# Fused matmul and RMS norm: a new order of evictions, copies and scalings at the end of the head, and a later scaling of row block 3

## The chip, the cores and the metric

The kernel runs on one core of one Trainium2 chip. The metric is device time in microseconds (us) of one execution. The engines are named as in the profile: PE is TensorE's matmuls and PEld its weight loads, DVE is VectorE, ACT is ScalarE, POOL is GpSimd, SP is SyncE, which here only issues DMAs.

## The reference

With a and b of 2048 x 2048 in float32, gamma of 2048 elements:

```python
x = np.matmul(a, b)
rms = np.sqrt(np.mean(x ** 2, axis=-1, keepdims=True) + eps)
return (gamma * x / rms).astype(np.float32)
```

Every row of the product is divided by its own root mean square, so a row can be scaled only when all of its 2048 columns are computed.

## The kernel before

The rows of a are cut into 16 blocks of 128 (0 to 15), the columns of b into halves of 1024 and chunks of 512. Blocks 0 to 3 are the **head**; they are multiplied while b is still being loaded. Blocks 4 to 15 follow in six **groups** of two row blocks (group 2 holds blocks 4 and 5, group 3 blocks 6 and 7, and so on), each worked off in two halves of b's columns. A group's half is computed with seven products instead of eight (a Strassen scheme in Winograd's form): a product is 8 matmuls of 128x128 by 128x512 into one PSUM bank, and its operands are sums and differences of quarters of a and b. The sums of b are made once, in the head (`b_diff`, `b_rest`); those of a once per group by `a_sums` on DVE (L323 to L330): sum 1 in place, sum 2 from sum 1, sum 3 from sum 2, sum 4 later. Product 7 uses sum 3, product 6 sum 2, product 5 sum 1, product 3 sum 4.

A row block from 4 on goes through these steps before PE can use it:

- `load_block` (L129) or `load_half`: a DMA on POOL's queue into one of two buffers of 1 MB. Block b uses the buffer of block b - 2, so its load cannot start before that block's scaling. `load_after` (L548) puts a one-element copy (L140) ahead of a load on POOL, which waits until a given transposed block has landed.
- `row_norm` (L217): two squares with a sum on ACT (L221) and a root (L224).
- `row_factor` (L227) and `row_apply` (L238) on DVE: four tiny operations that make a power of two, then one operation of 128x2048 (L240) that scales the block to float16.
- Transposing: blocks 4 and 5 on PE (`transpose_half`, L185, eight transposes of 128x128 into one bank), each half copied from PSUM by `take_transposed` (L195) on ACT or DVE; all later blocks by a DMA transposition on SP's queue (`transpose_dma`, L198).

The results go to tiles x of 128x1024. Products of the head's second pair of blocks (2 and 3) end in `pair_ends` (L505); plain products of blocks 0 and 1 are evicted by `evict` (L400). When a block's row is complete, `square_right` (L291) squares the right half on ACT and takes the root, to which `take_pre` (L276) has added the earlier part on DVE; `finish` (L301) then scales both halves with the inverse and gamma on DVE (L306, one per half) and stores each on SP's queue (L309).

Nothing here is scheduled by a planner: the program's order is the order of every engine's queue, and each engine works its queue strictly in order. What an instruction waits for, all behind it on its engine waits for too.

The places that the change touches:

- the head's end, L474 to L503: the last evictions of blocks 0 and 1, the norms and scalings of blocks 4 and 5, the products 6, 3, 5 and 4 of blocks 2 and 3 (right half), the transposes of blocks 4 and 5 and the first sums of group 2;
- `first_segment` (L552), the first half of group 2, where the load of block 8 is issued;
- `segment` (L578), where segment 1 (the second half of group 2) scales blocks 2 and 3 and makes the sums of group 3, which segment 2 needs first in its product 6.

PSUM has eight banks: tbank and acc_0 to acc_6; in the head's end acc_0 to acc_3 hold the plain products, u2 is acc_4, u4 acc_5, p7 acc_6.

Of the kernel before, what the change touches and what calls it, by code (L numbers as in the profile page):

```python
# [17 lines left out]
def kernel(  # L18
# [13 lines left out]
    nc = tc.nc  # L32
# [3 lines left out]
    KT = K // P  # L36
# [6 lines left out]
    HB = 4  # L43
    NG = MB // 2
    G0 = HB // 2
# [12 lines left out]
    tbank = psum.tile([P, CH], FP32, name="tbank")  # L58
    acc = [psum.tile([P, CH], FP32, name=f"acc_{n}") for n in range(7)]
# [22 lines left out]
    def a16_slot(mb):  # L82
        if mb == HB + 1:
            return a16_first
        if mb == HB:
            return x_slot[2 * HB - 1].bitcast(FP16)
        return head_flat.bitcast(FP16)[:, (2 + mb % 2) * K:(3 + mb % 2) * K]
# [3 lines left out]
    def at(mb):  # L91
        return (at_even, at_odd)[(mb // 2) % 2][:, mb % 2]
# [4 lines left out]
    def add(out, in0, in1, op=ALU.add):  # L97
        nc.vector.tensor_tensor(out=out, in0=in0, in1=in1, op=op)  # L98
# [30 lines left out]
    def load_block(mb):  # L129
        a32[mb] = a_pool.tile([P, K], FP32, name="a32")  # L130
        nc.gpsimd.dma_start(out=a32[mb], in_=a[mb * P:(mb + 1) * P, :])
# [53 lines left out]
    def transpose_half(mb, h, bank):  # L185
        view = bank.bitcast(FP16).rearrange("p (g m) -> p g m", m=P)
        for n in range(8):
            kt = h * 8 + n
            nc.tensor.matmul(
                view[:, n, :], a16[mb][:, kt * P:(kt + 1) * P], identity_h,  # L190
                is_transpose=True, start=(n == 0), stop=(n == 7),
            )
        return view

    def take_transposed(mb, h, view, copy):  # L195
        copy(out=at(mb)[:, h * 8:(h + 1) * 8, :], in_=view)
# [9 lines left out]
    def new_msq(mb):  # L206
        msq[mb] = msq_pool.tile([P, NCH + 1], FP32, name="msq")
        n_sq[mb] = 1
# [18 lines left out]
    def row_factor(mb):  # L227
        s = stat_pool.tile([P, 1], FP32, name="s")
        nc.vector.tensor_scalar_max(out=s, in0=norm.pop(mb), scalar1=1e-18)
        nc.vector.reciprocal(out=s, in_=s)  # L230
        nc.vector.tensor_single_scalar(out=s.bitcast(I32), in_=s.bitcast(I32),
                                       scalar=0x7F800000, op=ALU.bitwise_and)
        new_msq(mb)
        nc.vector.tensor_scalar(out=msq[mb][:, 0:1], in0=s, scalar1=s, scalar2=float(eps),
                                op0=ALU.mult, op1=ALU.mult)
        factor[mb] = s

    def row_apply(mb):  # L238
        a16[mb] = a16_slot(mb)
        nc.vector.tensor_scalar_mul(out=a16[mb], in0=a32.pop(mb), scalar1=factor.pop(mb))  # L240
# [29 lines left out]
    def square_half(mb, h):  # L270
        square_of(mb, x_tile(mb, h))
# [4 lines left out]
    def take_pre(mb):  # L276

        pre_of[mb] = stat_pool.tile([P, 1], FP32, name="pre")
        add(pre_of[mb], msq[mb][:, 0:1], msq[mb][:, 1:2])

    def root(last, part):
        rms = stat_pool.tile([P, 1], FP32, name="rms")
        nc.scalar.activation(out=rms, in_=last, func=ACTF.Sqrt, bias=part, scale=1.0)  # L283
        return rms
# [6 lines left out]
    def square_right(mb):  # L291

        square_half(mb, 1)
        rms_of[mb] = root(msq[mb][:, 2:3], pre_of.pop(mb))
# [6 lines left out]
    def finish(mb, order=(0, 1)):  # L301
        if mb not in inverse_of:
            inverse_of[mb] = inverse(rms_of.pop(mb))
        for h in order:
            x = x_half.pop((mb, h))
            nc.vector.scalar_tensor_tensor(  # L306
                out=x, in0=x, scalar=inverse_of[mb], in1=gamma_sb[:, h * HALF:(h + 1) * HALF],
                op0=ALU.mult, op1=ALU.mult)
            nc.sync.dma_start(out=rows(mb, h * HALF, (h + 1) * HALF), in_=x)  # L309
# [35 lines left out]
    def product_matmul(g, j, m, bank, kp, start):  # L345
        lhsT = {1: lambda: quarter(g, 0, 0), 2: lambda: quarter(g, 0, 1),
                3: lambda: sum_of(g, 4), 4: lambda: quarter(g, 1, 1), 5: lambda: sum_of(g, 1),
                6: lambda: sum_of(g, 2), 7: lambda: sum_of(g, 3)}[m]()
        rhs = {1: lambda: b_quarter(j, kp, 0, 0), 2: lambda: b_quarter(j, kp, 1, 0),
               3: lambda: b_quarter(j, kp, 1, 1), 4: lambda: sums[j][:, 2, kp, :],  # L350
               5: lambda: b_quarter(j, kp, 0, 1), 6: lambda: sums[j][:, 0, kp, :],
               7: lambda: sums[j][:, 1, kp, :]}[m]()
        nc.tensor.matmul(bank, lhsT[:, kp, :], rhs, start=(start and kp == 0),  # L353
                         stop=(kp == KP - 1), skip_group_check=not start)
# [45 lines left out]
    def evict(groups, engines):  # L400
        for g, engine in zip(groups, engines):
            copy_on(engine)(out=x_chunk(*g), in_=banks[g])  # L402
# [22 lines left out]
    plain = [(r, c) for r in range(2) for c in (2, 3)]  # L425
# [43 lines left out]
    r2, r3 = HB - 2, HB - 1  # L469
# [4 lines left out]
    b_rest(1, KP - 1)  # L474
    evict(plain[:2], "AD")
    row_norm(HB)
    for r in range(HB):
        take_pre(r)
    row_norm(HB + 1)
    product(PAIR, 1, 6, u2, start=False)  # L480
    nc.vector.tensor_copy(out=u4, in_=u2)
    evict(plain[2:3], "D")
    row_factor(HB)
    row_apply(HB)
    product(PAIR, 1, 3, acc[0])
    product(PAIR, 1, 5, u4, start=False)
    row_factor(HB + 1)
    row_apply(HB + 1)
    evict(plain[3:], "A")
    square_right(0)  # L490
    turned = [transpose_half(HB, 0, tbank)]
    for kp in range(KP):
        product_matmul(PAIR, 1, 4, u2, kp, False)
        if kp == 4:
            turned.append(transpose_half(HB, 1, acc[1]))
    load_block(HB + 3)
    take_transposed(HB, 0, turned[0], nc.scalar.copy)
    turned += [transpose_half(HB + 1, h, bank) for h, bank in enumerate((tbank, acc[2]))]
    square_right(1)
    take_transposed(HB, 1, turned[1], nc.vector.tensor_copy)  # L500
    take_transposed(HB + 1, 0, turned[2], nc.vector.tensor_copy)
    take_transposed(HB + 1, 1, turned[3], nc.scalar.copy)
    a_sums(G0, (3, 1, 2), False)  # L503

    def pair_ends():  # L505
# [42 lines left out]
    def load_after(src, mb):  # L548
        wait_for(src)
        load_block(mb)  # L550

    def first_segment():  # L552
        n, g, j = 0, G0, 0
        nxt = 2 * g + 2
        do(n, 1)
        do(n, 7, False)
        finish(0, (1,))
        pair_ends()
        do(n, 2)
        row_norm(nxt)  # L560
        a_sums(g, (4,))
        finish(0, (0,))
        do(n, 6)
        do(n + 1, 1)
        prepare(nxt)
        do(n, 5)
        nc.scalar.copy(out=chunks(n)[2], in_=B7)
        take(n, 22)
        row_norm(nxt + 1)
        take(n, 11)  # L570
        finish(1)
        do(n, 4)
        prepare(nxt + 1)
        load_after(at(nxt)[:, KT - 1, 0:1], nxt + 2)
        take(n, 21)
        square_half(2 * g + 1, j)

    def segment(n):  # L578
        g, j = halves[n]
        ra, rb, nxt = 2 * g, 2 * g + 1, 2 * g + 2  # L580
        more = g + 1 < NG
        do(n, 6)
        if j == 0:
            finish(ra - 1)
            if more:
                row_norm(nxt)
        elif g == G0:
            square_right(r2)
        do(n - 1, 3)
        take(n - 1, 12)  # L590
        if j == 0:
            square_right(ra - 2)
            if more:
                prepare(nxt)
            a_sums(g, (4,))
            finish(ra - 2)
        else:
            square_half(ra, 0)
            if g == G0:
                square_right(r3)  # L600
                for r in (r2, r3):
                    finish(r, (1, 0))
        do(n, 2)
        take(n, 11)
        do(n + 1, 1)
        if j == 0 and more:
            row_norm(nxt + 1)
        if j == 1 and g + 2 < NG:
            load_after(at(nxt + 1)[:, KT - 1, 0:1], nxt + 3)
        if j == 1 and more:  # L610
            a_sums(g + 1, (1, 2))
        do(n, 7)
        if j == 1 and more:
            a_sums(g + 1, (3,))
        do(n, 5)
        take(n, 22)
        if j == 1:
            take_pre(rb)
            take_pre(ra)
        do(n, 4)  # L620
        take(n, 21)
        if j == 0:
            square_half(rb, 0)
            if more:
                prepare(nxt + 1)
            if g + 2 < NG:
                load_after(at(nxt)[:, KT - 1, 0:1], nxt + 2)
        else:
            square_right(rb)

    def last_group():
        n = len(halves) - 2
# [137 lines left out]
```

## Time and profile before

| what | value |
|---|---|
| median of 3 runs | 226.18 us (225.19 to 226.31) |
| the profiled execution's own time | 224.53 us |
| its span, first to last instruction | 222.8 us |
| PE busy | 208.4 us, 94% |
| DVE busy | 144.6 us, 65% |
| ACT busy | 116.2 us, 52% |
| granted TensorE clock, mean | 0.992 |

Times in the timeline count from the span's start. A row of the timeline gives start, length, engine, line of the code, operation, what it writes and reads, how many instructions are merged, and in brackets the engine's idle time just before with what ended it. Matmuls are pipelined: a product's row is 1.89 us long, but the next product starts 1.72 to 1.73 us behind it; the distance of starts is what counts. A releaser is the one that came last by the profile.

### The profile page before, as it was taken

Reading aid. Unit: us, or ns where it says so; the run is one execution under the profiler, and the core shown is the slowest. Engines: PE = TensorE matmul, PEld = TensorE weight load, DVE = VectorE, ACT = ScalarE, POOL = GpSimd, SP = SyncE. Lnnn points to the kernel's source line nnn. Section 1 sums busy time; section 2 is a strip of 40 time slices with the busy share of each in tenths; the row PEclk is TensorE's granted clock in tenths of the full one; section 3 lists DMA queues with packets and bytes.
Section 4 is the critical chain, followed back from the end, with each engine's and each line's share of the span. In section 5 each row is a group of like instructions: output and inputs, shape, how many; then the busy total and the mean of one; then the engine's idle time right before and its main releaser. Section 6 shows DMA issues by size and latency. Waiting matters only on the chain.

```text
span 222.8 us, 2900 instructions
## 1 busy us (share of the span) xinstructions
PE 208.4 (94%) x1012; PEld 97.2 (44%) x1032; DVE 144.6 (65%) x281; ACT 116.2 (52%) x229; POOL 38.5 (17%) x74
## 2 busy tenths in 40 slices
PE   7799999999999999599999999999999999999970
PEld 3345544444444444244444444444444444444440
DVE  2128678999987994879616980678337963483381
ACT  2110003900797548569744965297726964364782
POOL 8544434433020011200110010200010000000030
PEclk9999999999999999999999999999999999999996
DMA  7999999999928489996885599547874875062044
GB/s 154 172 202 207 203 206 210 210 210 253 420 68 359 170 243 278 351 290 233 288 235 191 197 273 282 188 185 197 284 103 186 206 258 94 1 266 116 0 183 193
DMA packets 36719, 46.59 MB, mean 209 GB/s; under 512 B 22240, under 2 KB 26336, under 8 KB 35424
## 3 DMA queue, kind: packets, MB, share of 16 engines
q0 software_dynamic: 10608, 23.86, 43.9%
q1 hardware_dynamic: 25824, 22.29, 32.6%
q10 hardware_dynamic: 272, 0.26, 0.3%
q8 instruction: 8, 0.13, 0.2%
q14 instruction: 7, 0.06, 0.1%
HBM read 34.60 MB, written 16.78 MB: 231 GB/s over the span
## 4 chain that ended last, share of the span: by engine, by line
PE 53%; ACT 1%; issue 1%; DVE 1%; ACTq 0%
PE acc L353 53%; ACT sq L718 0%; ACT sq L267 0%; ACT a L645 0%; DVE s L330 0%; ACTq L765 0%; DVE head_at L330 0%; ACT rms L283 0%; DVE r L288 0%
## 5 line engine op out<-in xcount | busy, mean ns | idle before, releaser
L267 ACT ACTIVATE sq<-x 128x1024 bf16<-128x1024 f32 (+1 forms) x33 | 33.2, 1005 | 31.3 <-DVE x L98 27.5
L353 PEld LDWEIGHTS <-s 128*128 128x128 f16 (+1 forms) x312 | 30.4, 98 | 39.9 <-DVE s L330 3.5
L366 PE MATMUL acc<-b,head_at 128*128 128x512 bf16 x171 | 42.3, 379 | 1.5 <-DMA b<-in_b_dram 1.3
L353 PE MATMUL acc<-b,head_at 128*128 128x512 bf16 x164 | 40.8, 379 | 0.3
L306 DVE SCALAR_TENSOR_TENSOR x<-x,r,gamma_sb 128x1024 f32<-128x1024 f32 x28 | 34.8, 1282 | 0.5
L353 PE MATMUL acc<-b,at_even 128*128 128x512 bf16 x142 | 33.3, 379 | 0.1
L353 PEld LDWEIGHTS <-head_at 128*128 128x128 f16 (+1 forms) x216 | 21.0, 98 | 25.0
L353 PEld LDWEIGHTS <-at_even 128*128 128x128 f16 x192 | 18.8, 98 | 22.4
L353 PE MATMUL acc<-early,s 128*128 128x512 bf16 x108 | 27.1, 379 | 0.2
L366 PEld LDWEIGHTS <-head_at 128*128 128x128 bf16 x176 | 16.9, 97 | 20.6 <-issue 1.5
L221 ACT ACTIVATE sq<-a 128x1024 bf16<-128x1024 f32 x24 | 25.3, 1054 | 0.5
L353 PE MATMUL acc<-t_left,s 128*128 128x512 bf16 x95 | 22.5, 379 | 2.6 <-DVE s L330 2.4
L353 PE MATMUL acc<-b,s 128*128 128x512 bf16 x103 | 24.4, 379 | 0.1
L112 POOL DMA_DIRECT2D b<-in_b_dram x32 | 17.2, 541 | 20.6 <-DMA b<-in_b_dram 14.6
L98 DVE TENSOR_TENSOR x<-acc,x 128x512 f32<-128x512 f32 x23 | 15.9, 689 | 6.1 <-ACT x L534 3.3
L402 ACT COPY x<-acc 128x512 f32<-128x512 f32 x6 | 3.5, 583 | 25.6 <-PE acc L366 25.6
L240 DVE TENSOR_SCALAR head_at<-a,s 128x2048 f16<-128x2048 f32 x10 | 12.8, 1277 | 0.0
L288 DVE RECIPROCAL r<-rms 128x1 f32<-128x1 f32 x16 | 2.6, 161 | 12.8 <-ACT rms L283 12.7
L530 ACT COPY acc<-acc 128x512 f32<-128x512 f32 x12 | 6.9, 578 | 7.3 <-PE acc L353 7.3
L181 DVE COPY head_at<-tbank 128x1024 bf16<-128x1024 bf16 x7 | 4.8, 692 | 9.0 <-PE tbank L176 9.0
L330 DVE TENSOR_TENSOR at_even<-at_even 128x1024 f16<-128x1024 f16 x3 | 2.1, 692 | 12.5 <-DMA at_even<-head_at 12.5
L140 POOL CAST pace<-head_at 128x1 f32<-128x1 f16 x4 | 2.5, 620 | 43.6 <-DMA head_at<-head_at 43.6
(104 smaller groups left out, 208.1 us busy)
## 6 DMA issues: line engine op xcount, KB each, us to landing
out_dram<-x SPq DMA_DIRECT2D x29, 512.0 KB, 3.3
a<-in_a_dram POOLq DMA_DIRECT2D x10, 1024.0 KB, 5.9
b<-in_b_dram POOLq DMA_DIRECT2D x32, 256.0 KB, 10.1
a<-in_a_dram POOLq DMA_DIRECT2D x4, 512.0 KB, 9.8
early<-in_a_dram POOLq DMA_DIRECT2D x7, 256.0 KB, 10.2
gamma_sb<-in_gamma_dram POOLq DMA_DIRECT2D x2, 512.0 KB, 9.9
out_dram<-x SPq DMA_DIRECT2D x3, 256.0 KB, 2.5
out_dram<-a SPq DMA_DIRECT2D x1, 768.0 KB, 3.3
```

The source lines that it names most:

```text
L98: nc.vector.tensor_tensor(out=out, in0=in0, in1=in1, op=op)
L112: nc.gpsimd.dma_start(out=raw[j][kp][:, t, :], in_=b[lo:lo + P, j * HALF:(j + 1) * HALF])
L181: nc.vector.tensor_copy(out=head_at[:, 2 * kp:2 * kp + 2, :, :], in_=view)
L221: nc.scalar.activation(out=junk, in_=a32[mb][:, h * HALF:(h + 1) * HALF], func=ACTF.Square, scale=2.0 ** -8, accum_out=n2[:, h:h + 1])
L240: nc.vector.tensor_scalar_mul(out=a16[mb], in0=a32.pop(mb), scalar1=factor.pop(mb))
L267: nc.scalar.activation(out=sq[:, 0:src.shape[-1]], in_=src, func=ACTF.Square, scale=inv_sqrt_n, accum_out=msq[mb][:, c:c + 1])
L288: nc.vector.reciprocal(out=r, in_=rms)
L306: nc.vector.scalar_tensor_tensor(out=x, in0=x, scalar=inverse_of[mb], in1=gamma_sb[:, h * HALF:(h + 1) * HALF], op0=ALU.mult, op1=ALU.mult)
L353: nc.tensor.matmul(bank, lhsT[:, kp, :], rhs, start=(start and kp == 0), stop=(kp == KP - 1), skip_group_check=not start)
L366: nc.tensor.matmul(bank, head_at[:, kt, r, :], head_rhs(c, kt), start=(kt == 0), stop=(kt == KT - 1))
L402: copy_on(engine)(out=x_chunk(*g), in_=banks[g])
L530: nc.scalar.copy(out=b2, in_=b1)
```

## The change

At the head's end four things move:

- the four `take_pre` operations go from ahead of u4's copy on DVE to behind the copy of block 4's second half;
- the eviction of the third plain bank (`plain[2]`) goes from DVE, ahead of block 4's factor, to ACT, behind both norms; that of the fourth goes on ACT between the two `square_right`;
- the factor and scaling of block 5 follow those of block 4 directly in the program;
- block 4 is transposed in one go ahead of product 4, and block 5 within it (halves after 4 and 6 of its 8 matmuls), with both of its copies on DVE; before, block 4's second half lay within product 4 and block 5 behind it, with one copy on ACT.

In group 2, row block 3's `finish` moves from the middle of segment 1, ahead of the sums of group 3, to the end of that segment. In the first segment the load of block 8 waits for block 7's transposition in place of block 6's. No instruction is added or removed on any engine; only the order changes, and the engine of two copies (one from DVE to ACT, one from ACT to DVE).

```diff
     evict(plain[:2], "AD")
     row_norm(HB)
-    for r in range(HB):
-        take_pre(r)
     row_norm(HB + 1)
     product(PAIR, 1, 6, u2, start=False)
     nc.vector.tensor_copy(out=u4, in_=u2)
-    evict(plain[2:3], "D")
-    row_factor(HB)
-    row_apply(HB)
+    for mb in (HB, HB + 1):
+        row_factor(mb)
+        row_apply(mb)
+    evict(plain[2:3], "A")
     product(PAIR, 1, 3, acc[0])
     product(PAIR, 1, 5, u4, start=False)
-    row_factor(HB + 1)
-    row_apply(HB + 1)
+    turned = [transpose_half(HB, h, (tbank, acc[1])[h]) for h in range(2)]
+    take_transposed(HB, 0, turned[0], nc.scalar.copy)
+    take_transposed(HB, 1, turned[1], nc.vector.tensor_copy)
+    load_block(HB + 3)
+    for r in range(HB):
+        take_pre(r)
+    square_right(0)
     evict(plain[3:], "A")
-    square_right(0)
-    turned = [transpose_half(HB, 0, tbank)]
+    square_right(1)
     for kp in range(KP):
+        if kp in (4, 6):
+            h = kp // 2 - 2
+            view = transpose_half(HB + 1, h, (tbank, acc[2])[h])
+            take_transposed(HB + 1, h, view, nc.vector.tensor_copy)
         product_matmul(PAIR, 1, 4, u2, kp, False)
-        if kp == 4:
-            turned.append(transpose_half(HB, 1, acc[1]))
-    load_block(HB + 3)
-    take_transposed(HB, 0, turned[0], nc.scalar.copy)
-    turned += [transpose_half(HB + 1, h, bank) for h, bank in enumerate((tbank, acc[2]))]
-    square_right(1)
-    take_transposed(HB, 1, turned[1], nc.vector.tensor_copy)
-    take_transposed(HB + 1, 0, turned[2], nc.vector.tensor_copy)
-    take_transposed(HB + 1, 1, turned[3], nc.scalar.copy)
     a_sums(G0, (3, 1, 2), False)
...
@@ first_segment
         prepare(nxt + 1)
-        load_after(at(nxt)[:, KT - 1, 0:1], nxt + 2)
+        load_after(at(nxt + 1)[:, KT - 1, 0:1], nxt + 2)
         take(n, 21)
...
@@ segment
             if g == G0:
                 square_right(r3)
-                for r in (r2, r3):
-                    finish(r, (1, 0))
+                finish(r2, (1, 0))
         do(n, 2)
...
         else:
             square_right(rb)
+            if g == G0:
+                finish(r3, (1, 0))
```

## The prediction

> **What bounds the kernel now.** I read the busy table first, then the chain of work that ended last, then the list of waits, then the timeline around each place where TensorE (PE) stood still.
>
> ```profile
> PE 208.4 (94%) x1012; PEld 97.2 (44%) x1032; DVE 144.6 (65%) x281; ACT 116.2 (52%) x229; POOL 38.5 (17%) x74
> ```
>
> PE is busy 94% of the span; no other engine is near. The chain, in order of time (start, length, what):
>
> ```profile
> 93.16 0.60 DVE head_at L330
> ...
> 93.85 0.70 DVE s L330
> ...
> 94.60 9.46 PE acc L353 x43
> 104.05 0.05 issue
> 104.11 10.74 PE acc L353 x49
> ```
>
> From 94.60 to the final product PE runs without a wait (each further piece repeats "10.74 x49" with 0.05 between). So whatever moves PE's start at 94.60 moves the end, as long as nothing behind it becomes late. Ahead of 94.60 the chain is on VectorE (DVE), making operand sums. The waits (total, times, longest) name the gap:
>
> ```profile
> PE acc L353 <- DVE s L330: 2.4, 1, 2.4
> ```
>
> Around it, in the timeline:
>
> ```profile
> 83.60 0.53 POOL L131 DMA_DIRECT2D a<-in_a_dram  x1
> 83.69 5.01 SPq L199 DMA_TRANSPOSE head_at<-head_at  x1
> ...
> 90.27 1.89 PE L353 MATMUL acc<-early,at_even 128*128 128x512 bf16 x7
> ...
> 90.68 2.48 DVE L306 SCALAR_TENSOR_TENSOR x<-x,r,gamma_sb 128x1024 f32<-128x1024 f32 x2
> ...
> 93.07 0.68 DVE L330 TENSOR_TENSOR head_at<-head_at 128x1024 f16<-128x1024 f16 x1
> ```
>
> A product is 8 matmuls; neighbours start 1.725 us apart (88.54, 90.27). The next product should start at 90.27 + 1.725 = 92.00; it starts at 94.60: **2.60 us lost**. It needs sum 2 of blocks 6 and 7, two L330 operations. These start at 93.07, straight behind the scaling of row block 3 (L306, twice 1.28 us). Block 7's transposition (issued 83.69) landed at 91.2, so it was there by then. The head's end is the other place:
>
> ```profile
> 61.39 0.68 DVE L402 COPY x<-acc 128x512 f32<-128x512 f32 x1
> ...
> 61.67 1.89 PE L353 MATMUL acc<-b,head_at 128*128 128x512 bf16 x7
> ...
> 62.69 1.28 DVE L240 TENSOR_SCALAR x<-a,s 128x2048 f16<-128x2048 f32 x1
> ...
> 62.95 0.30 ACT L224 ACTIVATE norm<-n 128x1 f32<-128x1 f32 x1
> ...
> 64.02 0.62 PE L189 MATMUL tbank<-identity_h,x 128*128 128x128 f16 x8 [0.46 <-DVE s L229]
> ...
> 67.55 1.89 PE L353 MATMUL acc<-b,at_even 128*128 128x512 bf16 x7
> 67.75 1.01 ACT L196 COPY at_even<-acc 128x1024 f16<-128x1024 f16 x1 [0.38 <-PE acc L189]
> ...
> 69.54 1.90 PE L353 MATMUL acc<-t_left,s 128*128 128x512 bf16 x8
> ```
>
> Product 5 starts at 61.67 and frees PE at 63.39; the transposes of block 4 start at 64.02, when its scaling (L240, ends 63.97) is done: 0.63 us lost. The group's first product frees PE at 67.55 + 1.725 = 69.27; product 7 starts at 69.54, behind the copy of block 5 on ScalarE (ACT): 0.27 lost.
>
> **The change, part by part.**
>
> *DVE ahead of block 4.* Four L98 sums of 128x1 (60.52 to 60.79) and one eviction (0.60 to the next start) leave this place. The copy of u2 starts when the eviction at 59.92 is through, about 60.52 instead of 60.79. Factor 4 then starts 0.60 later, at 61.12 (norm 4 is there at 60.70), its scaling 0.70 after that, at 61.82, ending at 63.10. That is ahead of 63.39, so the 0.63 us stall goes. What is late next is block 5: its factor now meets norm 5, ready at 62.95 + 0.30 = 63.25, so it starts at 63.28 (before 63.88), scales from 63.98, and ends at 65.26.
>
> *PE.* Sixteen transposes of block 4 at 0.455 per eight: 63.39 to 64.30. Four matmuls of product 4 (0.216 each): to 65.17. Block 5's first half waits for 65.26 + 0.05 = 65.31: a new wait of 0.14, and queued behind it is all of PE. ScalarE's copy out of tbank (64.06 to 65.05) is done by then. Then 0.455, 0.43, 0.455, 0.43: product 4 ends at 67.08. Transposes between matmuls of an open accumulation are in the old trace too (65.56, pitch undisturbed), so I cost them at nothing beyond their time. The group's first product starts at 67.08 against 67.55: **0.47 gained**.
>
> *The copies.* DVE does block 4's second half at 65.17 to 65.86, the four moved sums to 66.1, block 5's first half at 66.05 (PE done 65.92) and its second at 66.84 (PE done 66.80) to 67.53. Sum 3 runs 67.55 to 68.24, product 7 wants it at 67.08 + 1.725 = 68.81. The 0.27 goes: **PE is 0.73 us ahead** from here (68.81 against 69.54). If the cover of 0.5 us is gone, that part comes back one for one. ACT has the moved eviction at 63.16, where it did another of 0.56 us before; its queue (copy 0.99, square and root 1.4, eviction 0.5, square and root 1.4) ends at about 68.4, and its next work waits for PE at 69.0. Nothing there is late. POOL's loads of blocks 6 and 7 follow the two scalings and move some 0.6 us forward.
>
> One row speaks against this stretch: the load of block 6 took 1.47 us to issue at 64.51, beside the scaling at 64.58, where its like take 0.53. The Trainium skill, "SBUF — State Buffer", section "SBUF: two separate sides", says that a VectorE operation in a two-port mode and GpSimd writing DMA descriptors shut each other out, whoever comes first. By it a load issued first could hold block 5's scaling 0.5 us, and the gain would be 0.5 us less; the row has that scaling at its usual 0.13 us behind its factor, so I charge nothing to DVE.
>
> *Row block 3's scaling behind the first group's last products.* This takes 0.20 + 2.48 us of DVE from ahead of the sums. Row block 2's scaling ended at 89.99; its cause is a chain over PE, DVE and ACT that moves with PE, so about 89.3. Sums 1 and 2 take 0.75 each: sum 2 at 90.8. PE wants it at 92.00 - 0.73 = 91.27. **All 2.60 us go**, if block 7 has landed by about 89.7.
>
> *The load of block 8* moves from ahead of block 7's transposition to behind its landing. The old trace has it at 83.60, with the transposition at 83.69, which took 7.5 us to land; the others took 4.3 to 6.8 (4.3 to 5.0 where no load ran beside them, 5.3 to 6.8 where one did). Without the load I take 4.3 to 5.5 (two stores are still in flight); the scaling of block 7 ends some 0.7 us earlier, so issue is near 82.95 and landing at 87.3 to 88.5. Loads 8 and 9 then go out together at about 88.5, where load 9 was at 91.95. Loads of 1 MB landed in 5.1 to 7.9 us: block 8 at 93.6 to 96.4. ACT reaches its squares at about 95.0 (98.67 before, of which 3.7 us go with the wait ahead of it). Late by nothing to 1.4 us; queued behind on ACT are the copies and squares of that segment. Their slack: the next products that wait for that chain are product 6 of the next half (copy ended 104.26, used 106.70) and product 6 of group 4 (sum 2 at 117.63, used 118.78). Shifted by 3.33 us, block 8 may be as late as 96.5 before PE waits. I take zero.
>
> *The scaling of block 3 at its new place* occupies DVE 93.0 to 95.6 and pushes the scaling of block 5 to 98.2; the norm of block 8 comes at 97.7. At most 0.6 us, under the slack above. Zero.
>
> **Sum.** 0.47 + 0.26 + 2.60 = 3.33 us. The profiled execution took 224.53 us with a span of 222.8, so 221.2 with 219.5. It is faster than all three timed runs; taken off their median: 226.18 - 3.33 = **222.9 us**.
>
> **Rivals.** (a) *Both stalls go*: 222.9, in 222.2 to 223.5. (b) *The transposition of block 7, or the chain to block 2's scaling, is the next wait.* For: without the move, landing at 82.95 + 7.5 = 90.45 gives sum 2 at 91.95, 0.7 late; block 2's scaling unmoved would give 0.2 to 0.7 late. Price 0.2 to 1.5: 223.1 to 224.6. (c) *Loads 8 and 9 collide with the stores of blocks 2 and 3* (windows 87 to 95 already move 331 to 360 GB/s): block 8 at 97 to 99, 0.5 to 2.5 lost: 223.4 to 225.4. (d) *The change doesn't do what it says*: sums still late by something not in the old trace (the 0.73 alone stays): 225.4. In the compiled order the sums stand ahead of block 3's scaling, so this is small. (e) *Slower*: load 8's wait on ACT is one for one behind 96.5, so it turns the sign at 96.5 + 3.33 = 99.8, that is 11.3 us after issue. The longest median landing of a group is 10.2 us, in the loading phase with many loads queued. At 102 it would be 226.18 - 3.33 + 5.5 = 228.4. By the skill's "TensorE: Matmul & The Clock Gate", "What's actually happening", an idle window of 3.4 us halves PE's clock; the 2.4 us gap here left it at 1.00, and no run here shows the longer one, which would come on top of (e).
>
> **How the numbers follow.** (a) 0.63, (b) 0.15, (c) 0.12, (d) 0.04, (e) 0.06. About 0.5% (1.1 us) is what timing can tell from no change, so faster means under 225.05: (a), (b) and two thirds of (c), 0.86; same 0.09; slower 0.05. The range 221.9 to 225.0 holds (a), (b) and most of (c), with some spread between runs.
>
> **What would show it.** In the new profile PE should not wait for L330; product 6 of group 3 should start near 91.3, behind its predecessor by 1.7; block 7 should land in under 6 us; ACT's squares of block 8 near 95 with no DMA named as releaser. A wait of ACT for the load of block 8 of over 1.5 us, followed by a PE wait for a copy or sum, would prove me wrong, as would a PE wait of over 0.3 us for block 5's scaling.

## The result, and the profile after

| | before | after |
|---|---|---|
| median | 225.69 us (4 runs, 224.59 to 226.31) | 223.12 us (4 runs, 222.88 to 223.24) |
| ratio, with its 95% interval | | 0.989 (0.9845 to 0.9935) |
| profiled execution, span | 222.8 us | 221.1 us |
| mean granted clock, profiled | 0.992 | 0.996 |

The forecast was 222.9 us, in a range of 221.9 to 225.0. Most executions of the kernel before, here and beside the experiments, fall into two groups, near 224.4 us at a mean granted clock of 0.991 to 0.995 and near 226.2 us at 0.984 to 0.987; the four of the changed kernel form one group, at 0.990 to 0.996. The two profiled means in the table differ only by the last fortieth of the span (0.6 and 0.8 there by the pages), where no matmul is left.

The profile after the head's end, in the timeline (start, length, engine, line, operation):

```profile
61.97 1.28 DVE L240 TENSOR_SCALAR x<-a,s 128x2048 f16<-128x2048 f32 x1
...
63.60 0.61 PE L189 MATMUL tbank<-identity_h,x 128*128 128x128 f16 x8
...
63.80 0.53 POOL L131 DMA_DIRECT2D a<-in_a_dram  x1 [8.98 <-DVE s L229]
...
64.18 1.28 DVE L240 TENSOR_SCALAR a_first<-a,s 128x2048 f16<-128x2048 f32 x1
...
65.52 0.62 PE L189 MATMUL tbank<-identity_h,a_first 128*128 128x128 f16 x8
...
67.29 1.89 PE L353 MATMUL acc<-b,at_even 128*128 128x512 bf16 x7
...
69.01 1.89 PE L353 MATMUL acc<-t_left,s 128*128 128x512 bf16 x8
```

This execution reached product 5 of the head at 61.87, 0.20 us later than the one before (61.67), so 0.20 is to be taken off. Block 4's transposes start 1.73 us behind product 5, without the wait of 0.63. Block 5's first half waits 0.17 for its scaling. Product 7 starts at 69.01 - 0.20 = 68.81, against 69.54: the 0.73 us of the forecast, at the very time it named.

At the start of group 3:

```profile
83.15 1.69 SPq L199 DMA_TRANSPOSE head_at<-head_at  x1
...
86.97 2.48 DVE L306 SCALAR_TENSOR_TENSOR x<-x,r,gamma_sb 128x1024 f32<-128x1024 f32 x2
...
88.25 0.53 POOL L131 DMA_DIRECT2D a<-in_a_dram  x1
...
89.37 0.69 DVE L330 TENSOR_TENSOR head_at<-head_at 128x1024 f16<-128x1024 f16 x1
...
89.73 1.89 PE L353 MATMUL acc<-early,at_even 128*128 128x512 bf16 x7
90.15 0.69 DVE L330 TENSOR_TENSOR s<-head_at 128x1024 f16<-128x1024 f16 x1
...
91.46 1.89 PE L353 MATMUL acc<-t_left,s 128*128 128x512 bf16 x8
```

Sum 1 follows the scaling of row block 2 directly, and product 6 starts 1.73 us behind its predecessor: the whole 2.60 us are gone here. But the list of waits still has one of PE for a sum:

```profile
ACT sq L221 <- DMA a<-in_a_dram: 1.2, 1, 1.2
PE acc L353 <- DVE s L330: 1.0, 1, 1.0
```

It is at another place, one group later:

```profile
96.21 1.06 ACT L221 ACTIVATE sq<-a 128x1024 bf16<-128x1024 f32 x1 [1.18 <-DMA a<-in_a_dram]
...
100.95 3.78 SPq L199 DMA_TRANSPOSE at_even<-head_at  x1
...
103.55 1.89 PE L353 MATMUL acc<-early,s 128*128 128x512 bf16 x8
...
104.89 1.49 DVE L98 TENSOR_TENSOR x<-acc,x 128x512 f32<-128x512 f32 x2 [0.81 <-ACT x L532]
105.63 1.89 PE L353 MATMUL acc<-b,s 128*128 128x512 bf16 x8 [0.20 <-DVE x L98]
...
107.49 0.89 POOL L131 DMA_DIRECT2D a<-in_a_dram  x1 [0.37 <-DVE msq L234]
...
108.33 5.22 SPq L199 DMA_TRANSPOSE at_even<-head_at  x1
...
114.26 1.89 PE L353 MATMUL acc<-early,head_at 128*128 128x512 bf16 x8
115.59 0.69 DVE L330 TENSOR_TENSOR at_even<-at_even 128x1024 f16<-128x1024 f16 x1 [7.32 <-DMA at_even<-head_at]
...
116.37 0.69 DVE L330 TENSOR_TENSOR s<-at_even 128x1024 f16<-128x1024 f16 x1
...
117.12 1.90 PE L353 MATMUL acc<-t_left,s 128*128 128x512 bf16 x8 [0.97 <-DVE s L330]
```

The same place in the kernel before, where neither product waits:

```profile
106.70 1.89 PE L353 MATMUL acc<-early,s 128*128 128x512 bf16 x8
...
108.42 1.89 PE L353 MATMUL acc<-b,s 128*128 128x512 bf16 x8
108.44 0.53 POOL L131 DMA_DIRECT2D a<-in_a_dram  x1 [0.37 <-DVE x L98]
...
110.78 3.73 SPq L199 DMA_TRANSPOSE at_even<-head_at  x1
...
117.06 1.89 PE L353 MATMUL acc<-early,head_at 128*128 128x512 bf16 x8
...
118.78 1.89 PE L353 MATMUL acc<-t_left,s 128*128 128x512 bf16 x8
```

Read the changed kernel's rows from the top: ScalarE waits for block 8's load until 96.2. Product 3 of group 3's first half starts at 105.63 in place of 103.55 + 1.73 = 105.28, 0.35 us late, for an addition that stands behind ScalarE's delayed queue. Block 9's transposition goes out at 108.33, 0.84 us behind the load of block 10 (2.34 before); it lands 7.2 us later (5.3 before), sum 2 is done at 117.06, and product 6 of group 4 starts at 117.12 in place of 114.26 + 1.73 = 115.99: 1.13 us late. The account of the two profiled executions: - 0.73 - 2.60 + 0.20 + 0.35 + 1.13 = - 1.65 us; the spans differ by 1.7.

So three questions: is it the later load that gives 1.5 us back, or the later scaling of row block 3? By what road? And why did the medians differ by 2.6 us where the profiles differ by 1.7?

### The profile page after: what moved, and what is told of

Its sections match the earlier page's. It is cut to its first block, busy times and chain, and to the rows that moved or that the text cites. A ratio compares the mean times of both kernels' runs of the same rounds, so it can differ in the third digit from the quotient of the medians.

```text
span 221.1 us, 2897 instructions
## 1 busy us (share of the span) xinstructions
PE 208.3 (94%) x1012; PEld 97.4 (44%) x1032; DVE 144.4 (65%) x281; ACT 115.7 (52%) x229; POOL 37.7 (17%) x74
## 4 chain that ended last, share of the span: by engine, by line
PE 65%; issue 11%; DMA 10%; ACT 7%; DVE 3%; POOL 1%; ACTq 0%; POOLq 0%; DVEq 0%
PE acc L353 46%; PE acc L366 15%; ACT sq L221 4%; DMA a<-in_a_dram 4%; DMA at_even<-head_at 3%; DMA early<-in_a_dram 3%; PE tbank L392 2%; PE tbank L176 2%; ACT sq L267 1%; DVE a_first L240 1%; POOL b L112 0%; ACT norm L224 0%; ACT sq L717 0%; POOL pace L140 0%; ACT a L644 0%
## 5 line engine op out<-in xcount | busy, mean ns | idle before, releaser
L402 ACT COPY x<-acc 128x512 f32<-128x512 f32 x7 | 4.1, 580 | 25.5 <-PE acc L366 25.5
L695 POOL TENSOR_SCALAR x<-x,r 128x512 f32<-128x512 f32 x1 | 1.9, 1852 | 46.5 <-DVE r L288 46.5
L288 DVE RECIPROCAL r<-rms 128x1 f32<-128x1 f32 x16 | 2.6, 160 | 10.8 <-ACT rms L283 10.7
```

## The experiments

**The parts of the change, one at a time.** Three kernels have one part each, a fourth all but the load:

```diff
# e1: the changed kernel, with both of these taken back
# e2: the kernel before, with the first alone
# e3: the kernel before, with the second alone
# e4: the changed kernel, with the second taken back
-                for r in (r2, r3):
-                    finish(r, (1, 0))
+                finish(r2, (1, 0))
...
+            if g == G0:
+                finish(r3, (1, 0))
# second:
-        load_after(at(nxt)[:, KT - 1, 0:1], nxt + 2)
+        load_after(at(nxt + 1)[:, KT - 1, 0:1], nxt + 2)
```

> The kernel before with the head's end of the change alone (block 3's scaling and block 8's load where they were). Theory: PE is 0.7 us ahead from product 7 of the first group on, the wait ahead of product 6 of group 3 stays near 2.6 us because the chain to block 3's scaling moves with PE, and nothing later waits: 0.7 us under before, some 0.3%. Rival: that chain does not move with PE, so the wait grows by 0.7 us and the gain is nil.

> The kernel before with block 3's scaling moved alone. Theory (the later waits of the changed kernel come from block 8's late load): sum 2 waits for block 7's transposition, which lands near 91.2 beside block 8's load, so product 6 of group 3 starts near 92.7 in place of 94.6 and nothing later waits: 1.9 us under before. Rival (they come from block 3's scaling lying ahead of the scalings of blocks 5 and 8): the same start, then a wait of about 1 us ahead of product 6 of group 4, and 0.9 us under before.

> The kernel before with block 8's load behind block 7's landing, alone. Theory: block 7 lands in 4.3 to 5 us, but block 3's scaling still holds sum 1 until 93.1; block 8 lands near 96, ahead of ScalarE's square at 98.7; no new wait, time as before within 0.3 us. Rival (a late load is a loss by itself, whatever stands ahead): product 6 of group 4 waits about 1 us, time 1 us over before.

> The changed kernel with block 8's load put back behind block 6's landing. Theory (late load costs the 1.5 us lost in product 3 and product 6 of groups 3 and 4): both of those waits go; block 7 lands in about 7.5 us, so product 6 of group 3 waits about 0.7 us: 0.7 us under the changed kernel, 222.4 us. Rival (block 3's later scaling costs them): they stay, with the 0.7 us on top: 223.8 us.

| | median us | span, profiled | ratio to before |
|---|---|---|---|
| before | 224.53 | 222.8 | |
| head's end alone | 224.13 | 221.9 | 0.9991 (0.9952 to 1.003) |
| block 3's scaling alone | 222.54 | 220.7 | 0.9891 (0.9837 to 0.9945) |
| block 8's load alone | 224.84 | 222.8 | 1.0015 (0.9978 to 1.0052) |
| all but the load | 221.83 | 219.8 | 0.9852 (0.9801 to 0.9904) |

The head's end alone leaves the wait of 2.60 us as it was and takes 0.9 us off the span (0.14 of it from an earlier start of the head); the ratio of the medians is within what can be told from no change. Among the executions at a mean clock of 0.991 or more, its median is 223.97 us (6 of 10) against 224.45 (13 of 19), some 0.5 us less. With block 3's scaling alone, the timeline of PE has

```profile
90.04 1.89 PE L353 MATMUL acc<-early,at_even 128*128 128x512 bf16 x7
92.56 1.68 PE L353 MATMUL acc<-t_left,s 128*128 128x512 bf16 x7 [0.63 <-DVE s L330]
```

that is, 92.56 - 91.77 = 0.79 us in place of 2.60, and no wait after it: the rival, a wait in group 4, is not there. The load alone does nothing to the time: block 7's transposition lands in 4.3 us, block 8's load takes 7.7, and PE still waits 2.44 by the profile's count, for DVE. In the kernel with all but the load, the same two products of PE:

```profile
89.38 1.89 PE L353 MATMUL acc<-early,at_even 128*128 128x512 bf16 x7
91.70 1.04 PE L353 MATMUL acc<-t_left,s 128*128 128x512 bf16 x4 [0.43 <-DVE s L330]
```

It waits 0.60 us, since block 7's transposition lands in 7.3, and nowhere after. It is 1.3 us faster than the changed kernel (0.7 were expected): 1.48 - 0.60 = 0.88 us of that are the waits of the two traces, and 0.35 an earlier start of the head in the profiled execution. So block 3's scaling costs nothing later, and **the late load costs more than it brings**: 0.60 us saved at product 6 of group 3, 1.48 lost behind.

**The load in between.** Block 8's load let go 2.3 us behind the transposition's issue, where ScalarE has squared the left half of block 5:

```diff
-        load_after(at(nxt + 1)[:, KT - 1, 0:1], nxt + 2)
         take(n, 21)
         square_half(2 * g + 1, j)
+        load_after(msq[2 * g + 1][:, 1:2], nxt + 2)
```

> The changed kernel with block 8's load let go in between: behind ScalarE's square of block 5's left half (near 85 us), 2 us behind the issue of block 7's transposition and 2.5 us ahead of its landing. Theory (only the two ends are bad: beside the whole transposition, or behind it): block 7 lands by 89.4, in time for sum 1, block 8 by 93, no wait of PE ahead of product 6 of groups 3 and 4: 1.5 us under the changed kernel, 221.6 us. Rival (any overlap costs the transposition its full 3 us): product 6 of group 3 waits 0.4 to 0.7 us as with the load at its old place: 221.9 us, no better than that kernel.

221.80 us, ratio 0.9839 (0.9794 to 0.9883). Its timeline:

```profile
83.45 1.71 SPq L199 DMA_TRANSPOSE head_at<-head_at  x1
...
85.72 0.53 POOL L131 DMA_DIRECT2D a<-in_a_dram  x1 [0.32 <-issue]
...
87.85 0.76 POOL L140 CAST pace<-head_at 128x1 f32<-128x1 f16 x1 [1.60 <-DMA head_at<-head_at]
```

The transposition landed in 4.3 us although the load was issued 2.0 us ahead of that, so the rival's wait did not come. But the two did not overlap, so the run does not show that overlap is free. Of the DMA packets that the trace holds, the transposition's (256 bytes each) run from 84.6 to 87.2, and the load's (8 KB each) begin at 87.3. In the kernel before, with the load issued 0.09 us ahead, the load's run from 84.9 to 88.7, and nine tenths of the transposition's come behind that, up to 90.8. The two take turns, and what holds up a transposition is a load whose packets go first. Group 3 starts without a wait, and ScalarE finds block 8 there. But block 9's load, still issued at 88.55 into the stores of row block 2, took 9.3 us; block 8's transposition took 5.3, block 9's 7.5, and product 6 of group 4 waited 0.33 by the profile. So the gain at one place is eaten at the other, and this kernel and the one with all but the load are equal within what timing tells. Both are faster than the changed kernel. There is no measurement of a version with block 9's load moved as well.

**The road of the loss.** The changed kernel without the two stores of row block 3 (`finish` gets a switch for its stores):

```diff
-                finish(r3, (1, 0))
+                finish(r3, (1, 0), False)   # scaled, not stored
```

> The changed kernel without the two stores of row block 3, so those 128 rows of the result are left unwritten (1 MB less to move); the scaling itself stays. Theory (the late loads of blocks 8 and 9 and the stores crowd the DMA engines, which delays block 8's transposition, then block 10's load, which meets block 9's transposition): block 8's transposition lands in 4.3 to 4.6 us in place of 5.9, block 9's in under 6.3 in place of 7.2, and the 1.1 us wait ahead of product 6 of group 4 shrinks below 0.3 us: 222.1 us. Rival (ScalarE's late squares of block 8 alone carry it): the wait stays near 1 us, time within 0.3 us of the changed kernel.

221.74 us. The transpositions of blocks 8 and 9 landed in 4.3 and 5.5 us in place of 5.9 and 7.2, the wait ahead of product 6 of group 4 is gone, though ScalarE waited as long as ever for block 8 (1.3 us). The wait ahead of product 3 stayed:

```profile
105.61 1.89 PE L354 MATMUL acc<-b,s 128*128 128x512 bf16 x8 [0.28 <-DVE x L98]
```

So the two losses have two roads. The 0.35 us come over ScalarE's queue, from block 8's late landing. The 1.13 us come over the DMA engines: loads 8 and 9 are still under way (7.9 and 10.7 us to landing) when the stores of blocks 2, 3 and 5 come, all that holds up block 8's transposition, with it block 10's load, and that goes ahead of block 9's transposition. The packets of the changed kernel, with those of the kernel without the two stores in brackets, show each step: loads 8 and 9 from 90.9 to 99.2 (91.0 to 99.8), the stores behind them up to 104.3 (102.4), block 8's transposition from 103.0 to 106.3 (102.2 to 104.7), load 10 from 109.6 to 113.0 (107.9 to 111.3), block 9's transposition up to 115.1 (113.4), with nine tenths of it behind load 10. Both are needed for the loss: it is gone without the two stores, and gone with the stores and an early load.

**Within the head's end: block 5 within product 4, or behind it.**

```diff
     for kp in range(KP):
-        if kp in (4, 6):
-            h = kp // 2 - 2
-            view = transpose_half(HB + 1, h, (tbank, acc[2])[h])
-            take_transposed(HB + 1, h, view, nc.vector.tensor_copy)
         product_matmul(PAIR, 1, 4, u2, kp, False)
+    for h in range(2):
+        view = transpose_half(HB + 1, h, (tbank, acc[2])[h])
+        take_transposed(HB + 1, h, view, nc.vector.tensor_copy)
```

> The changed kernel with block 5 transposed behind product 4 in place of within it. Theory: what the head's end gains is the earlier start of block 4's scaling and the copies on VectorE; without the split PE no longer waits 0.17 us for block 5's scaling, product 1 of the first group starts 0.2 us earlier, but sum 3 is ready only at about the time product 7 wants it, so product 7 starts within 0.15 us of where it did: same time. Rival (putting the transposes within product 4 is what hides block 5's copies): product 7 waits 0.5 us or more for sum 3, and the kernel is that much slower.

223.18 us (the changed kernel: 223.12).

```profile
61.59 1.89 PE L353 MATMUL acc<-b,head_at 128*128 128x512 bf16 x8
...
66.83 1.89 PE L353 MATMUL acc<-b,at_even 128*128 128x512 bf16 x8
68.73 1.90 PE L353 MATMUL acc<-t_left,s 128*128 128x512 bf16 x8
```

From product 5 to product 7 it is 68.73 - 61.59 = 7.14 us, and 69.01 - 61.87 = 7.14 in the changed kernel (7.87 before). Product 1 starts earlier and product 7 waits for sum 3 instead. The split that the change puts into product 4 earns nothing; what is left of the head's change, the earlier scaling and the copies on VectorE, earns the 0.73 (the two weren't taken apart). The loads and stores behind the head are those of the changed kernel, and the two later losses in this trace are 0.24 and 1.60 us, where they were 0.35 and 1.13: the size of that loss differs from execution to execution.

**The two groups of executions.** Of the 42 executions of the kernel before that ran beside these kernels, 17 had a mean clock of 0.977 to 0.987 (6 of 19 in one set, which the expectation below counts as seven, and 11 of 23 in the other); of the 20 of the two kernels that keep the long wait, 8; of 32 executions of the six kernels without it (the changed one among them), none. First, the wait filled with matmuls, then the wait by itself:

```diff
+        if n == 2:
+            for _ in range(9):
+                nc.tensor.matmul(tbank, identity_h, sums[0][:, 0, 0, :], start=True, stop=True)
         do(n, 6)
```

> The kernel before with nine matmuls whose result nobody reads put into PE's wait ahead of product 6 of group 3 (1.94 of 2.60 us); everything else as before. Seven of 19 executions of the kernel before, and 8 of 20 of the two kernels that keep this wait, took 1.6 to 2 us longer at a mean granted clock of 0.984 to 0.987 in place of 0.991 to 0.995; none of 12 executions of kernels without the wait did. Theory: the wait itself lets the clock drop in some executions; filled, no execution is in the upper group, all near 224.4 us. Rival: the upper group has nothing to do with the wait; some 4 in 10 executions stay near 226.2 us.

224.49 us; one execution of 12 had the lower clock (0.982, 226.45 us), another took 225.53 at 0.994. Fewer, but not none: 0.50 us of wait were left by the profile, and what let the clock drop in that one execution stays open. There is no measurement of the kernel before with the whole wait filled, or with a longer one. So a kernel that does nothing but matmuls with such waits between them, one execution for each length of the wait, on another chip:

```python
for gap in range(GAPS + 1):
    count = 58 + (gap * 7) % 16
    for n in range(count):
        nc.tensor.matmul(acc[n % 8], first if n == 0 else w[:, n % 8, :], rhs[:, n % 4, :],
                         start=True, stop=True)
    last = acc[(count - 1) % 8]
    nc.vector.tensor_copy(out=x, in_=last)
    ...
    for _ in range(ADDS):                     # 0, 2 and 4
        nc.vector.tensor_tensor(out=x, in0=x, in1=y, op=ALU.add)
    nc.vector.tensor_copy(out=first, in_=x[:, 0:P])
```

> A kernel of its own, which computes nothing of the reference: 15 stretches of 58 to 73 matmuls of 128x512 on random data, between them 14 waits in which VectorE copies the last bank and 128x128 of it back as PE's next operand, near 1.1 us each. Theory (a wait of some length lets PE's granted clock drop): after waits this short no stretch shows a clock under 1.00 nor slow matmuls behind its start. Rival (the lower clock of some executions has nothing to do with waits): the same here; the next two kernels tell.

> As the kernel with short waits, with two more operations of VectorE in each, so that PE waits 2.6 us, as ahead of product 6 of group 3 in the kernel before. Theory: some 4 in 10 of the 14 waits (17 of 42 executions of the kernel before had the lower mean clock), between 2 and 9, are followed by a stretch of lower clock, which costs 1.6 to 2 us. Rival: none is.

> As the kernel with short waits, with four more operations of VectorE in each, waits of 4.0 us. Theory: more of the 14 waits, 8 or more, are followed by a stretch of lower clock. Rival: none is.

| wait of PE by the profile, us | waits followed by a slow stretch | extra time of such a stretch, us | mean clock |
|---|---|---|---|
| 1.05 | 0 of 14 | | 1.000 |
| 2.50 | 10 of 14 | 1.46 to 1.70 | 0.938 |
| 3.95 | 14 of 14 | 1.47 to 2.96 | 0.889 |

(Extra time: the distance to the next wait, less 0.2157 us a matmul and the wait.) Where a stretch is slow, the timeline and the windows (stretch; length; then PE, PEld, DVE and POOL, each busy us and instructions; then the clock) show it in the kernel with waits of 2.50 us:

```profile
98.88 0.39 PE L57 MATMUL acc<-rhs,first 128*128 128x512 bf16 x1 [2.50 <-DVE first L65]
99.11 14.80 PE L57 MATMUL acc<-rhs,w 128*128 128x512 bf16 x59
116.41 0.39 PE L57 MATMUL acc<-rhs,first 128*128 128x512 bf16 x1 [2.50 <-DVE first L65]
```

```profile
88.00:96.00 8.00, 7.95 (x37) 3.63 (x37) 0.00 (x0) 0.00 (x0) 1.00 0.00 0
98.90:102.30 3.40, 3.40 (x11) 1.28 (x12) 0.00 (x0) 0.00 (x0) 0.63 0.02 5
102.30:105.70 3.40, 3.35 (x14) 1.49 (x14) 0.00 (x0) 0.00 (x0) 0.87 0.00 0
```

Behind the wait the clock is at 0.63, then 0.87 over the next stretch, and 1.00 later. These are means: in stretches of 1 us of the same trace the clock is 0.50 from 100 to 103 and 1.00 again from 104.

The clock records of the traces say when a wait does this. Each drop is a stretch at 0.50 of 3.41 us (6.83 us after six of the waits of 3.95), and within a trace the drops start whole multiples of 3.41 us apart. Lay that grid over the waits of 2.50 and 3.95 us: in each of the 24 that were followed by a drop, PE was idle for 2.06 us or more within one cell of the grid, and the drop began with the next cell; in the four without a drop the most in one cell was 1.97. So the drop depends on how the wait falls on the grid, and a wait of 1.05 us can't reach the limit anywhere. The profiled executions of the three kernels with a wait of 2.44 us fit: their grid, taken from the drop behind the last matmul, leaves at most 1.57 (before), 1.81 (head's end alone) and 1.36 us (block 8's load alone) in one cell, and no drop follows the wait.

A wait as long as the one ahead of product 6 of group 3 thus drops the clock often and not always. Half the clock for 3.41 us costs 1.71 us and takes 0.008 off the mean clock of some 224 us, which is what lies between the two groups of the kernel before (1.75 us; 0.993 and 0.985). In that kernel itself the drop was not seen in a trace, since the traces taken of it are of the other group; that it is the same drop follows from the equal cost, the equal loss of mean clock and its absence in the kernels without the wait, and is otherwise argued.

## Why the prediction was right, and where it was not

- **Head's end, 0.73 us:** right, step by step: product 7 came at 68.81 when put on the same start. The new wait for block 5's scaling was forecast at 0.14 and was 0.17. That the gain is 0.73 rests on the one trace of the kernel before: from product 5 to product 7 the old order took 7.87, 7.69, 7.78 and 7.53 us in four traces (before, block 3's scaling alone, block 8's load alone, wait filled), the new order 7.14 in all six. So the gain is 0.39 to 0.73, in the mean 0.58.
- **Wait ahead of product 6 of group 3, 2.60 us:** right. Sum 1 started behind row block 2's scaling (89.37, or 89.17 on the same start, forecast 89.3), with block 7 landed in 4.2 us.
- **SBUF's port pair:** the load of block 6 now issues at 63.80, ahead of block 5's scaling, takes 0.53 in place of 1.47 us, and the scaling starts 0.13 behind its factor as ever. The 0.5 us that the Trainium skill's rule ("SBUF — State Buffer", section "SBUF: two separate sides") would have had VectorE lose were not lost.
- **The load of block 8, "I take zero": the step that failed.** The landing was forecast at 93.6 to 96.4 and came at 96.2; ScalarE's wait was to be up to 1.4 us and was 1.18. Yet the bound "as late as 96.5 before PE waits" was wrong, and 1.48 us were lost inside it. By shifting the old times it took the later transpositions at their old durations (4.3 and 5.3 us); with loads 8 and 9 and the stores all behind each other they took 5.9 and 7.2. And the list of what waits on that chain missed product 3, whose bank is freed by an addition behind ScalarE's copy. This was rival (c), the collision with the stores, with a smaller delay of the load than it asked for (96.2, not 97 to 99) and most of the loss on a road that it did not name, over the transpositions.
- **Rival (b)** would have been the price of not moving the load: 0.60 us with the head's end, 0.79 without (forecast 0.7 for the landing at 90.45). The upper end of its range, 224.6, doesn't follow from its price: 222.85 + 1.5 = 224.35.
- **The base.** The sum of 3.33 us was taken off the median of 226.18, which belonged to the group with the dropped clock. Against the profiled execution it was 1.7 us, not 3.33. That the median came within 0.2 us of the forecast all the same is luck: the base lay 1.65 us above the profiled execution (226.18 and 224.53), and the profiled gain fell 1.68 us short of the sum. The change also removes the second group, some 1.75 us in 17 of 42 executions, which was not foreseen. And the four executions of the kernel before that the result compares with lay high: with the 19 and 23 executions of it beside the experiments, medians 224.53 and 224.80, the changed kernel's 223.12 is 1.4 to 1.7 us faster, not 2.6.
- **The clock.** The prediction said that the 2.4 us gap left the clock at 1.00. The one trace showed that; other executions of the same kernel had the lower mean clock, and by the kernels of waits alone the same length drops it in 10 of 14 cases.

## What to carry to other kernels

A transfer taken out of the way of one step lands on the next: before moving a load, write down what else will be in flight when it goes out and which of the two goes first, take the transfers behind it at their crowded durations and not at their quiet ones, and list every instruction queued behind each engine that will wait. When one trace disagrees with the median of the runs, look at the mean clock of each execution before using either as a base. A wait of the matmul engine of some 2.5 us can cost more than its length, so removing it may pay more than the trace shows, even if a wait of about 1 us comes elsewhere.

## What the runs showed of the hardware

- After PE waits of 2.50 us its granted clock dropped in 10 of 14 cases, after 3.95 us in all 14, after 1.05 us in none; each drop cost 1.5 us or more. In these traces it came where PE was idle for 2.06 us or more in one cell of a grid of 3.41 us, and not at 1.97 us or less. The Trainium skill, "TensorE: Matmul & The Clock Gate", section "What's actually happening", has the clock fall to half after an idle window of about 3.4 us; here it fell after 2.5 us too, so the measurement decides: a wait need not be as long as that window.
- A DMA transposition of one block took 4.2 to 4.4 us to land with little beside it, 7.2 to 7.7 with a 1 MB load issued up to 1 us ahead of it, and 4.3 with the load issued 2.3 us after it. By the packets, the transposition and the load took turns: the one whose packets came first was through, or nearly so, before the other's moved.
